# Solving RWKV's two right-hand sides in one run of products, loading two small weights a step ahead, and moving one merge behind the transitions

## The chip, the cores and the metric

One core of one Trainium2 chip runs the whole kernel. The metric is the device time of an execution in microseconds (us); lower is better. TensorE multiplies, DVE (VectorE) and ACT (ScalarE) read its results out of PSUM, POOL (GpSimd) does a little, SP (SyncE) issues most transfers.

## What is computed

A decoder block in float32 on 16 meta tokens and 1024 tokens of width 1024: a SwiGLU FFN at half step, a mixing stage, an output projection, a second FFN. The mixing stage adds two branches, A (gated DeltaNet, 8 heads of 128) and B (RWKV-7, 16 heads of 64). Cut to those:

```python
u = _rmsnorm(h, mix_norm[l])
aq, ak, av, az, abeta, aalpha, bcols, ga, gb = jnp.split(u @ w_in[l], ...)
# A, by chunks of 64 tokens:
tinv = lax.linalg.triangular_solve(m + eye, eye, left_side=True, lower=True, unit_diagonal=True)
# B, token by token (here also done by chunks of 64):
sa = jnp.einsum('bhvk,bhk->bhv', state, a_t)
state = state * w_t[:, :, None, :] + sa[..., None] * b_t[:, :, None, :] \
    + v_t[..., None] * k_t[:, :, None, :]
y_t = jnp.einsum('bhvk,bhk->bhv', state, r_t)
merged = jax.nn.sigmoid(ga) * o_a + jax.nn.sigmoid(gb) * o_b
h = h + merged @ w_out[l]
```

## The kernel before

The first FFN, the mixing stage, the output projection and the second FFN run one behind another. The mixing stage is done in two segments of the sequence (528 and 512 tokens) and in each of them in 8 steps; a step is one group of heads, one of A and two of B. 16 steps in all, numbered 0 to 15. Each step projects its inputs (the long products `pp`, 128x512, and `pw`, `pa` out of the small up-projection weights), then builds chunk operands, inverts small triangular matrices, and walks the chunks.

What is traced in which order stands in `schedule()`: a step's `merge_blocks`, `transitions`, `chains`, `gates` and `finish` are mixed with the next step's `operands` and `inverses` and with `new_b` and `new_a` of a later step. A list scheduler then sets each engine's order, so that work of several steps stands mixed in each queue, and each engine runs its queue strictly in that order.

Names that the text uses:

- `new_b`, `new_a` project; `gates` projects the output gates (`zg`). `new_b` loads `upr` (the up-projection weights of B) and `gates` loads `ugr` by SP and splits them on ACT and DVE into `upz` and `ug`. Any 128x1024 weight block is split in the same way into `w` (L159 on ACT, then L160 on DVE) once the block that was in the buffer has been read by its last `pp`.
- `operands`: `grb` are the score products of 64x128, which DVE masks into `LT`; `gra` those of A, which DVE makes into `UA` and `attn`; `bkt` transposes give `BKt`; the run `vp` gives `at` (a transposed AR) and `yb`; `ktp`, `btp` transpose for A and the meta tokens.
- `inverses` and `merge_blocks` invert by blocks into `Y`: the products `iv1` to `iv4`; iv3 gives `T64` through ACT, iv4 completes the inverse of A (the order prints all of them as iv with a number).
- `transitions` solves with B's part of `Y`: `xp` from `at` gives `xa`, `xp` from `LT`, `Vs` and then from that result gives `xv`, `vp` gives `vbk`. Then `mp` (matrices `mt` and `AR`, added up by DVE) and `np` (added to `vbk` and `yb` by DVE).
- `chains` walks the chunks (`b`, `p`, `pq`, `bm`, `am`).

Products with 64 rows and 64 columns use one quadrant of the array; where two quadrants on the diagonal are used, two run at a time. In the trace each float32 product of this kind has two records.

PSUM pools: `ch` has two banks, used in turn by xp, mp, np, iv and the transitions' vp; `mx` has two banks in the first segment and three in the second, used by `operands`. A tile there waits until the one before it in its bank has been read.

Of the kernel before, what the change touches and what calls it, by code (L numbers as in the profile page):

```python
# [185 lines left out]
BEFORE_SWITCH = "merge_blocks transitions operands+ inverses+ chains gates finish gates+ segment new_b++ new_a++"
SWITCH = "merge_blocks transitions operands+ inverses+ chains finish new_b++ new_a++"
LAST_BUT_ONE = "merge_blocks transitions operands+ inverses+ chains gates finish"
FINAL = "gates merge_blocks transitions chains fill finish"
# [1216 lines left out]
def transitions(g, q):  # L1406
# [3 lines left out]
    AR, LT, BKt, Vs, yb = q.AR, q.LT, q.BKt, q.Vs, ch3(q.yb, CB)  # L1410
    vbk = q.vbk = st.tile([P, NCB, CB], F32, name="vbk", tag="vbk")
    xa, xv = (st.tile([P, NCB, CB], F32, name=x, tag=x) for x in ("xa", "xv"))

    vka = q.at

    def solved(r):
        def f(i, h):
            t = tok(i, h)
            return Y[HS[t], i, HS[t]], r[HS[t], i], t, t
        return f  # L1420
# [7 lines left out]
    def va(i, h):  # L1428
        k = key(i, h)
        return LT[HS[k], i, 1 - (i & 1), :CB], Vs[HS[k], i], k, 1 - k  # L1430

    def vb(i, h):
        k = key(i, h)
        return BKt[HS[k], i, 1 - (i & 1)], Vs[HS[k], i], k, h
# [241 lines left out]
```

## Time and profile before

| | us |
|---|---|
| median of 3 runs | 3091.28 (3090.76 to 3095.39) |
| profiled execution | 3088.92 |
| its span, first to last instruction | 3087.2 |
| TensorE busy in the span | 2976.7 |

The profiled execution is the one that every row below comes from. A row of the timeline gives the start, the duration (of several alike: from the first's start to the last's end), the engine, the line, and what is written out of what; brackets give the engine's idle time just before it and what ended that. Busy times of TensorE rest on modelled ends of its instructions.

### The profile page before, as it was taken

How to read it: one execution, taken by the hardware profiler on the slowest of the kernel's cores; microseconds unless marked ns; L12 is line 12 of the kernel's file. 1: busy time of each engine (PE TensorE's matmuls, PEld its weight loads, DVE VectorE, ACT ScalarE, POOL GpSimd, SP SyncE). 2: the span in 40 equal slices, each digit the busy share in tenths (PEclk: the TensorE clock that was granted, in tenths of full speed). 3: DMA queues.
4: the chain of work that ended last, by engine and by line, in shares of the span. 5: the costliest groups of instructions: out<-in, count | busy, mean ns of one | idle time of the engine just before them, and what ended most of it. 6: DMA issues, size and time to landing. Idle time of an engine off the chain costs nothing.

```text
span 3087.2 us, 61391 instructions
## 1 busy us (share of the span) xinstructions
PE 2976.7 (96%) x25498; PEld 2538.9 (82%) x25498; DVE 1923.9 (62%) x3742; ACT 1326.2 (43%) x2308; POOL 330.3 (11%) x519
## 2 busy tenths in 40 slices
PE   8999999999899999999999999999999999999998
PEld 8999998998778888888777777777777888887886
DVE  6455453346667777677767777777766755555335
ACT  5322222126555645556565554555544432222114
POOL 0222220000000000000000000000000022332000
PEclk9999999999999999999999999999999999999999
DMA  3232224234223322233322232223345132224223
GB/s 126 80 97 83 83 86 157 79 100 140 62 74 77 81 71 70 73 79 88 93 78 73 78 87 82 73 71 85 101 134 190 64 102 89 82 82 170 86 77 114
DMA packets 257591, 287.17 MB, mean 93 GB/s; under 512 B 169296, under 2 KB 175440, under 8 KB 257312
## 3 DMA queue, kind: packets, MB, share of 16 engines
q1 hardware_dynamic: 253072, 271.43, 29.3%
q0 software_dynamic: 2512, 8.65, 0.7%
q8 instruction: 201, 3.29, 0.4%
q10 hardware_dynamic: 1728, 3.16, 0.3%
q14 instruction: 78, 0.64, 0.1%
HBM read 232.70 MB, written 50.47 MB: 92 GB/s over the span
## 4 chain that ended last, share of the span: by engine, by line
PE 58%; DVE 7%; ACT 5%; DMA 2%; issue 2%; SPq 1%; DVEq 0%; POOL 0%; ACTq 0%
PE pp L262 20%; PE pg L450 12%; PE pd L262 7%; PE pwo L262 2%; PE cs L1000 2%; PE pg L474 1%; PE b L1520 1%; PE vp L1035 1%; DVE w L160 1%; PE mp L1035 1%; PE gra L1230 1%; PE np L1035 1%; DVE acc L1151 1%; ACT w L159 1%; PE xp L1035 1%
## 5 line engine op out<-in xcount | busy, mean ns | idle before, releaser
L262 PE MATMUL pp<-uk,w 128*128 128x512 f32 (+2 forms) x4824 | 979.8, 351 | 5.4 <-DVE w L160 3.6
L262 PEld LDWEIGHTS pp<-uk,w 128*128 128x128 f32 x4824 | 742.0, 190 | 121.6 <-issue 32.2
L159 ACT ACTIVATE w<-wraw 128x1024 fp32r<-128x1024 f32 (+2 forms) x330 | 326.1, 989 | 723.5 <-PE pd L262 293.0
L262 PE MATMUL pd<-hd,w 128*128 128x512 f32 (+2 forms) x2640 | 498.5, 351 | 13.8 <-DVE w L160 9.8
L262 PEld LDWEIGHTS pd<-hd,w 128*128 128x128 f32 x2640 | 430.2, 190 | 81.0 <-DVE w L160 11.8
L160 DVE TENSOR_TENSOR w<-wraw,w 128x1024 fp32r<-128x1024 f32 (+2 forms) x330 | 376.1, 1140 | 88.4 <-ACT w L159 84.3
L450 PE MATMUL pg<-bt,w 128*128 128x256 f32 (+2 forms) x2520 | 404.0, 318 | 0.1
L456 DVE TENSOR_TENSOR c<-c,pg 128x520 f32<-128x520 f32 (+1 forms) x280 | 189.4, 690 | 336.2 <-PE pg L450 277.4
L450 PEld LDWEIGHTS pg<-bt,w 128*128 128x128 f32 x2520 | 361.1, 188 | 32.9 <-DVE w L160 0.3
L450 PE MATMUL pg<-b,w 128*128 128x256 f32 (+2 forms) x2160 | 348.1, 318 | 0.2 <-DVE c L456 0.2
L450 PEld LDWEIGHTS pg<-b,w 128*128 128x128 f32 x2160 | 309.9, 188 | 28.3 <-PE pg L450 0.4
L419 POOL TENSOR_TENSOR wrx<-wrx 128x512 f32<-128x512 f32 x38 | 57.2, 1504 | 759.0 <-DVE w22b L160 340.6
L1342 DVE TENSOR_TENSOR tb<-Ub,Xb 115x126 f32<-115x126 f32 (+22 forms) x496 | 124.9, 252 | 14.9 <-DMA Ub<-scr 6.4
L1344 DVE TENSOR_TENSOR Xb<-Xb,tb 115x126 f32<-115x126 f32 (+22 forms) x496 | 125.6, 253 | 9.3
L1151 DVE SCALAR_TENSOR_TENSOR acc<-xr,pk,acc 128x528 f32<-128x528 f32 (+1 forms) x144 | 109.2, 759 | 26.6 <-ACT acc L1147 24.9
L159 ACT ACTIVATE w<-wrx 128x1024 fp32r<-128x1024 f32 (+1 forms) x64 | 58.2, 909 | 157.0 <-PE pg L450 152.0
L609 DVE SCALAR_TENSOR_TENSOR h<-pd,h 128x528 f32<-128x528 f32 (+1 forms) x64 | 44.6, 699 | 118.8 <-PE pd L262 118.8
L609 DVE SCALAR_TENSOR_TENSOR hh<-pd,hh 128x512 f32<-128x512 f32 x64 | 44.2, 690 | 112.6 <-PE pd L262 108.7
L262 PE MATMUL pwo<-uk,w 128*128 128x512 f32 x384 | 98.2, 405 | 5.5 <-ACT uk L159 2.0
L918 ACT ACTIVATE sh<-pp,pk 128x528 f32<-128x528 f32 (+1 forms) x54 | 37.5, 694 | 126.1 <-PE pp L262 118.7
L262 PEld LDWEIGHTS pwo<-uk,w 128*128 128x128 f32 x384 | 71.6, 191 | 23.4 <-ACT uk L159 2.4
L159 ACT ACTIVATE hd<-hr 128x1040 fp32r<-128x1040 f32 (+1 forms) x44 | 45.3, 1060 | 67.4 <-DMA hr<-hid 42.5
(389 smaller groups left out, 3999.8 us busy)
## 6 DMA issues: line engine op xcount, KB each, us to landing
wraw<-in_win SPq DMA_DIRECT2D x150, 512.0 KB
wraw<-in_wgu SPq DMA_DIRECT2D x44, 512.0 KB
wrx<-in_wgu SPq DMA_DIRECT2D x44, 512.0 KB
wraw<-in_wdn SPq DMA_DIRECT2D x48, 320.0 KB
wraw<-in_wdn SPq DMA_DIRECT2D x32, 384.0 KB
hid<-c SPq DMA_DIRECT2D x44, 260.0 KB
hr<-hid SPq DMA_DIRECT2D x22, 520.0 KB
hid<-c SPq DMA_DIRECT2D x44, 256.0 KB
```

What stands on the lines that cost most here:

```text
L159: g.nc.scalar.activation(hi, src, AF.Copy)
L160: (eng or g.nc.vector).tensor_tensor(lo, src, hi.bitcast(F32), op=ALU.subtract)
L262: g.nc.tensor.matmul(ps, lhsT=l, rhs=r, start=i == 0, stop=i == n - 1)
L419: sums.tensor_tensor(a22, a21, a22, op=ALU.add)
L450: nc.tensor.matmul(ps[:, c0 : c0 + cn], lhsT=l[:, x, k, :], rhs=r[:, k, y, c0 : c0 + cn], start=i == 0, stop=i == 3 * HK - 1)
L456: nc.vector.tensor_tensor(o, x, y, op=ALU.add)
L609: nc.vector.scalar_tensor_tensor(hv, pd, 0.5, hv, op0=ALU.mult, op1=ALU.add)
L1000: nc.tensor.matmul(ps[:, :cn], lhsT=lhsT, rhs=sq[:, c0 : c0 + cn], start=True, stop=True)
L1035: g.nc.tensor.matmul(ps[e][HS[dst], c0 : c0 + CB], lhsT=l, rhs=r, start=True, stop=True)
L1151: nc.vector.scalar_tensor_tensor(acc[:, :n], xr[:, tap : tap + n], V("convw", ct * 4 + tap), acc[:, :n], op0=ALU.mult, op1=ALU.add)
L1342: nc.vector.tensor_tensor(tv, U[:, i, i + 1 :].unsqueeze(2).to_broadcast([npt, nt, ncc]), X[:, i, 0:ncc].unsqueeze(1).to_broadcast([npt, n ...
L1344: nc.vector.tensor_tensor(X[:, i + 1 :, 0:ncc], X[:, i + 1 :, 0:ncc], tv, op=ALU.add)
```

## The change

Four edits:

- `operands` now makes both right-hand sides of B's solve, side by side in one tile `rh`: the old `at` and the product of LT and Vs. It also makes the product of BKt and Vs into `vbk`. Both runs of products moved there from `transitions`, out of pool `ch` into `mx`.
- `transitions` solves both in one run `xp` of 16 products of 64x128 (before: 32 of 64x64 in two runs, one right-hand side behind the other) and two evictions of 128x512 into `xav` in place of four of 128x256.
- The up-projection weights of step n+1 are loaded when those of step n have been split, into tiles of their own (`upw_load`, `upw_next`).
- iv3, T64 and iv4 leave `merge_blocks` for `merge_a`, which is traced behind `transitions`.

`vbk` gets two buffers and `BKt` one, and a scratch of `finish` lies in AR in place of BKt.

```diff
-REGULAR = "merge_blocks transitions operands+ inverses+ chains gates finish new_b++ new_a++"
+REGULAR = "merge_blocks transitions merge_a operands+ inverses+ chains gates finish new_b++ new_a++"
...
+def upw_load(g, name, it):
+
+    if it < 2 * NJ:
+        raw = g.st.tile([P, 2, P], F32, name=name, tag=name)
+        g.nc.sync.dma_start(raw, g.a[name][it % NJ])
+        g.upw[name, it] = raw
...
-    raw = tmp("upr", 512).rearrange("p (a m) -> p a m", m=P)
-    nc.sync.dma_start(raw[:, 0:2, :], g.a["upwa"][j])
+    raw = upw_next(g, "upwa", it)
...
+    upw_load(g, "upwa", it + 1)
...
+    rh = q.rh = st.tile([P, NCB, 2, CB], F32, name="rh", tag="rh")
...
     for ps, cs in pa:
-        nc.scalar.activation(at[:, cs], ps, AF.Copy)
+        nc.scalar.activation(rh[:, cs, 0], ps, AF.Copy)
     for ps, cs in pr:
         nc.scalar.activation(ch3(yb, CB)[:, cs], ps, AF.Copy)
+    for ps, cs in run(g, g.mx, "vp", va)[0]:
+        nc.scalar.activation(rh[:, cs, 1], ps, AF.Copy)
+    for ps, cs in run(g, g.mx, "vp", vb)[0]:
+        nc.scalar.activation(vbk[:, cs], ps, AF.Copy)
...
+def merge_a(g, q):
...
     ps3 = g.ch.tile([P, 512], F32, name="iv3", tag="ch")
...
+    x = st.tile([P, NCB, 2, CB], F32, name="xav", tag="xav")
+    for cs in EO:
+        ps = g.ch.tile([P, 512], F32, name="xp", tag="ch")
+        for n, i in enumerate(range(cs.start, NCB, 2)):
+            for hp in HS:
+                nc.tensor.matmul(ps[hp, n * P : n * P + P], lhsT=Y[hp, i, hp],
+                                 rhs=q.rh[hp, i].rearrange("p a b -> p (a b)"), start=True, stop=True)
+        nc.scalar.activation(x[:, cs], ps.rearrange("p (c x b) -> p c x b", x=2, b=CB), AF.Copy)
...
-    px, pv = run(g, g.ch, "xp", solved(q.at), va)
-    for ps, cs in pv:
-        nc.scalar.activation(vka[:, cs], ps, AF.Copy)
-    for ps, cs in px:
-        nc.scalar.activation(xa[:, cs], ps, AF.Copy)
-    for ps, cs in run(g, g.ch, "xp", solved(vka))[0]:
-        nc.scalar.activation(xv[:, cs], ps, AF.Copy)
-    for ps, cs in run(g, g.ch, "vp", vb)[0]:
-        nc.scalar.activation(vbk[:, cs], ps, AF.Copy)
```

TensorE's queue around a step's transitions in the first segment, steps 1 to 5 alike (line numbers of the one kernel and of the other differ). Before:

```order
L1035 MATMUL xp<-at,Y_7139 64x64 x14
L1035 MATMUL vp<-Vs,BKt 64x64 x8
L1189 MATMUL grb<-AR,BK 64x128
L1035 MATMUL vp<-Vs,BKt 64x64 x8
L1035 MATMUL mp<-BKt,xa 64x64 x16
L1035 MATMUL mp<-LT,xa 64x64 x16
L1189 MATMUL grb<-AR,BK 64x128 x4
L262 MATMUL pp<-uk,w 128x512 x7
L1035 MATMUL np<-xv,BKt 64x64 x16
L1035 MATMUL np<-LT,xv 64x64 x16
L1189 MATMUL grb<-AR,BK 64x128 x16
L1476 MATMUL bm_13083<-uvm_7155,ltm 16x64 x2
```

and after:

```order
L1451 MATMUL xp<-rh,Y_7139 64x128 x7
L1038 MATMUL mp<-BKt,xav 64x64 x8
L1038 MATMUL mp<-LT,xav 64x64 x7
L1038 MATMUL mp<-BKt,xav 64x64 x8
L1038 MATMUL mp<-LT,xav 64x64 x9
L1204 MATMUL grb<-AR,BK 64x128 x16
L262 MATMUL pp<-uk,w 128x512
L1038 MATMUL np<-xav,BKt 64x64 x16
L1038 MATMUL np<-LT,xav 64x64 x16
L1204 MATMUL grb<-AR,BK 64x128 x16
L1430 MATMUL iv_12709<-XA,UA 64x64 x4
L262 MATMUL pp<-uk,w 128x512 x3
```

Seven pp and four grb stood between mp and np, now one pp and sixteen grb; the two merge products, which stood ahead of xp in before, now stand behind np where bm was.

DVE's queue in the same step. Before:

```order
L160 TENSOR_TENSOR w<-wraw,w 128x1024
L160 TENSOR_TENSOR ug<-ugr,ug 128x128
L1544 TENSOR_TENSOR ug<-ugr,ug 32x128
L1057 TENSOR_TENSOR upz<-upr,upz 64x128 x2
L1450 TENSOR_TENSOR mt<-mp,ck 64x4x64 x4
L1453 TENSOR_TENSOR AR<-mp,AR 128x4x64 x2
L1192 TENSOR_TENSOR LT<-grb,ck 128x4x128 x2
L1456 TENSOR_TENSOR vbk<-np,vbk 128x4x64 x2
L1459 TENSOR_TENSOR yb<-np,yb 128x4x64
L1457 TENSOR_TENSOR vbk<-vbk,gam 128x512
```

and after:

```order
L1233 TENSOR_TENSOR kts<-gp,tk 128x4
L1466 TENSOR_TENSOR mt<-mp,ck 64x4x64 x4
L1469 TENSOR_TENSOR AR<-mp,AR 128x4x64 x2
L1207 TENSOR_TENSOR LT<-grb,ck 128x4x128 x2
L160 TENSOR_TENSOR w<-wraw,w 128x1024
L1472 TENSOR_TENSOR vbk<-np,vbk 128x4x64 x2
L1475 TENSOR_TENSOR yb<-np,yb 128x4x64
L1473 TENSOR_TENSOR vbk<-vbk,gam 128x512
L1475 TENSOR_TENSOR yb<-np,yb 128x4x64
```

The split of a weight block into w, which DVE did ahead of mt, now stands between LT and the sum into vbk.

TensorE's queue in the second segment, steps 9 to 14 alike but for a few products. Before, from mp on:

```order
L1035 MATMUL mp<-LT,xa 64x64 x16
L1189 MATMUL grb<-AR,BK 64x128 x11
L1230 MATMUL gra<-kq 128x256 x2
L1035 MATMUL np<-xv,BKt 64x64 x16
L1035 MATMUL np<-LT,xv 64x64 x16
L1230 MATMUL gra<-kq 128x256 x2
L1259 MATMUL bkt<-ck,BK 64x64 x32
L1520 MATMUL b_22471<-SBs,mt 128x64
L1035 MATMUL vp<-ck,AR 64x64 x16
L1035 MATMUL vp<-LT,Vs 64x64 x16
L1285 MATMUL ktp<-ck,kq 128x128 x4
```

and after:

```order
L1038 MATMUL mp<-LT,xav 64x64 x9
L1204 MATMUL grb<-AR,BK 64x128 x17
L1038 MATMUL np<-xav,BKt 64x64 x16
L1038 MATMUL np<-LT,xav 64x64 x16
L1204 MATMUL grb<-AR,BK 64x128 x11
L1430 MATMUL iv_21975<-XA,UA 64x64 x4
L1204 MATMUL grb<-AR,BK 64x128 x4
L1435 MATMUL iv_21982<-Y_7139,T_21976 64x64 x4
L1245 MATMUL gra<-kq 128x256 x4
L1274 MATMUL bkt<-ck,BK 64x64 x32
L1038 MATMUL vp<-ck,AR 64x64 x16
```

Two gra left the gap between mp and np and grb came in; the merge products follow np, and two more runs of vp precede ktp.

ACT's queue at the transitions in the second segment. Before:

```order
L1440 ACTIVATE xa<-xp 128x4x64 x2
L1438 ACTIVATE at<-xp 128x4x64 x2
L159 ACTIVATE ug<-ugr 128x128
L1542 ACTIVATE ug<-ugr 128x128
L1055 ACTIVATE upz<-upr 128x256
L1442 ACTIVATE xv<-xp 128x4x64 x2
L1444 ACTIVATE vbk<-vp 128x4x64 x2
```

and after:

```order
L930 ACTIVATE zg<-pp 128x512
L159 ACTIVATE w<-wraw 128x1024
L1179 ACTIVATE Va<-vap 128x512
L1453 ACTIVATE xav<-xp 128x4x128
L1231 ACTIVATE E<-E 128x512
L1453 ACTIVATE xav<-xp 128x4x128
L1232 ACTIVATE eg<-gp 128x512
L1234 ACTIVATE kts<-kts 128x4
```

The splits of ug and upz no longer stand ahead of the eviction that the next products need; they now stand further down, in the chains.

TensorE's queue at `operands` in the first segment, from the end of the vp run on. Before:

```order
L1035 MATMUL vp<-LT,Vs 64x64 x16
L1500 MATMUL p_13109<-SA,kq 128x128
L262 MATMUL pp<-uk,w 128x512 x3
L1280 MATMUL btp<-ck,bkm 64x128
L1285 MATMUL ktp<-ck,kq 128x128 x4
```

and after:

```order
L1038 MATMUL vp<-LT,Vs 64x64 x16
L1516 MATMUL p_13077<-SA,kq 128x128
L262 MATMUL pp<-uk,w 128x512 x3
L1038 MATMUL vp<-Vs,LT 64x64 x16
L1038 MATMUL vp<-Vs,BKt 64x64 x8
L1520 MATMUL p_13081<-rhA,Y_7139 128x128
L1038 MATMUL vp<-Vs,BKt 64x64 x8
L1309 MATMUL btp<-ck,bkm 64x128
L1524 MATMUL pq<-kq,SA 128x128
L1525 MATMUL pq<-attn,vn 128x128
L1314 MATMUL ktp<-ck,kq 128x128 x4
```

LT times Vs and BKt times Vs stand between vp and btp, with p of the chains in between.

## Rows read from the trace of the kernel before

**Rows 1.** Page, part 1: busy time, share of the span, instructions

```profile
PE 2976.7 (96%) x25498; PEld 2538.9 (82%) x25498; DVE 1923.9 (62%) x3742; ACT 1326.2 (43%) x2308; POOL 330.3 (11%) x519
```

**Rows 2.** Stretches: us, each engine's busy time (instructions), PEclk, DMA share, GB/s

```profile
978.30:1460.90 482.60, 470.45 (x5637) 400.04 (x5636) 352.19 (x865) 265.54 (x546) 30.10 (x115) 1.00 0.28 75
...
1677.10:2289.40 612.30, 584.55 (x6436) 460.12 (x6435) 452.90 (x1081) 331.02 (x635) 39.19 (x99) 0.99 0.31 85
```

**Rows 3.** Waits of PE: line waited for, total us, times, longest

```profile
PE vp L1035 <- ACT xv L1442: 12.1, 14, 2.4
...
PE xp L1035 <- ACT at L1438: 7.7, 14, 0.9
...
PE np L1035 <- DVE AR L1453: 6.1, 13, 1.5
...
PE vp L1035 <- DVE attn L1234: 3.7, 5, 1.1
```

**Rows 4.** Groups by form, PE: records | busy us, mean ns | idle before

```profile
L1189 PE MATMUL grb<-AR,BK 64*64 64x128 f32 x1024 | 59.5, 282 | 0.0
...
L1035 PE MATMUL xp<-at,Y 64*64 64x64 f32 x1024 | 39.7, 222 | 7.8 <-ACT at L1438 7.7
```

**Rows 5.** Timeline of PE, transitions of a step in the first segment

```profile
1271.33 0.27 PE L1035 MATMUL xp<-at,Y 64*64 64x64 f32 x2 [0.89 <-ACT at L1438]
...
1273.46 0.68 PE L1035 MATMUL vp<-Vs,BKt 64*64 64x64 f32 x16 [0.25 <-ACT xv L1442]
...
1275.92 1.88 PE L262 MATMUL pp<-uk,w 128*128 128x512 f32 x7
1278.06 0.86 PE L1035 MATMUL np<-xv,BKt 64*64 64x64 f32 x27 [0.25 <-DVE AR L1453]
...
1279.49 1.09 PE L1189 MATMUL grb<-AR,BK 64*64 64x128 f32 x28
1280.79 0.38 PE L1476 MATMUL bm<-uvm,ltm 16*16 16x64 f32 x4 [0.21 <-DVE yb L1459]
```

**Rows 6.** Timeline of DVE, the same step

```profile
1271.05 1.23 DVE L160 TENSOR_TENSOR w<-wraw,w 128x1024 fp32r<-128x1024 f32 x1 [0.78 <-ACT w L159]
...
1275.74 1.73 DVE L1450 TENSOR_TENSOR mt<-mp,ck 64x256 f32<-64x256 f32 x4 [2.37 <-PE mp L1035]
1277.48 0.76 DVE L1453 TENSOR_TENSOR AR<-mp,AR 128x256 f32<-128x256 f32 x2
1278.16 1.28 DVE L1192 TENSOR_TENSOR LT<-grb,ck 128x512 f32<-128x512 f32 x2
1279.56 0.76 DVE L1456 TENSOR_TENSOR vbk<-np,vbk 128x256 f32<-128x256 f32 x2
1280.23 0.42 DVE L1459 TENSOR_TENSOR yb<-np,yb 128x256 f32<-128x256 f32 x1
1280.56 0.68 DVE L1457 TENSOR_TENSOR vbk<-vbk,gam 128x512 f32<-128x512 f32 x1
```

**Rows 7.** Timeline of ACT, that step's operands: evictions behind the vp run

```profile
1292.20 0.66 ACT L1274 ACTIVATE at<-vp 128x256 f32<-128x256 f32 x2 [1.50 <-PE vp L1035]
1292.74 0.67 ACT L1276 ACTIVATE yb<-vp 128x256 f32<-128x256 f32 x2
```

**Rows 8.** Timeline of ACT, transitions of a step in the second segment

```profile
1948.83 0.31 ACT L159 ACTIVATE ug<-ugr 128x128 fp32r<-128x128 f32 x1 [1.83 <-DMA ugr<-in_upg]
...
1949.55 0.64 ACT L1442 ACTIVATE xv<-xp 128x256 f32<-128x256 f32 x2
```

**Rows 9.** Timeline of PE, the same step

```profile
1950.24 0.68 PE L1035 MATMUL vp<-Vs,BKt 64*64 64x64 f32 x16 [1.59 <-ACT xv L1442]
...
1953.14 1.13 PE L1230 MATMUL gra<-kq 128*128 128x256 f32 x4
1954.83 0.86 PE L1035 MATMUL np<-xv,BKt 64*64 64x64 f32 x27 [0.56 <-DVE AR L1453]
...
1959.61 0.88 PE L1035 MATMUL vp<-ck,AR 64*64 64x64 f32 x30 [0.78 <-DVE attn L1234]
```

**Rows 10.** Timeline of PE, the step behind the switch of segments

```profile
1687.50 0.97 PE L1035 MATMUL np<-xv,BKt 64*64 64x64 f32 x27 [1.46 <-DVE AR L1453]
```

More of the change, by code (lines that the diff above doesn't have):

```diff
@@ L184 @@
 FIRST = "new_b new_a operands inverses", "new_b new_a"
-REGULAR = "merge_blocks transitions operands+ inverses+ chains gates finish new_b++ new_a++"
[L186 to L189, printed above, removed]
+REGULAR = "merge_blocks transitions merge_a operands+ inverses+ chains gates finish new_b++ new_a++"
+BEFORE_SWITCH = "merge_blocks transitions merge_a operands+ inverses+ chains gates finish gates+ segment new_b++ new_a++"
+SWITCH = "merge_blocks transitions merge_a operands+ inverses+ chains finish new_b++ new_a++"
+LAST_BUT_ONE = "merge_blocks transitions merge_a operands+ inverses+ chains gates finish"
+FINAL = "gates merge_blocks transitions merge_a chains fill finish"
 def weight_order():
@@ L816, in middle @@
             nc.gpsimd.memset(t, 0.0)
+        g.upw = {}
+        for name in ("upwa", "upg"):
+            upw_load(g, name, 0)
         steps = {}
@@ L1037, in run, with upw_next @@
     return out
+def upw_load(g, name, it):
[3 more added lines that the diff above has]
+        g.upw[name, it] = raw
+def upw_next(g, name, it):
+    return g.upw.pop((name, it))
 def new_b(g, it):
@@ L1251, in operands @@
     inverse_inputs(g, q)
-    BKt = q.BKt = st.tile([P, NCB, 2, CB], F32, name="BKt", tag="BKt", bufs=2)
+    BKt = q.BKt = st.tile([P, NCB, 2, CB], F32, name="BKt", tag="BKt")
     ident = g.C("ident")
@@ L1270, in vr, with vb @@
         return Vs[HS[k], i], LT[HS[k], i, 1 - (i & 1), CB:], k, h
+    def vb(i, h):
+        k = key(i, h)
+        return BKt[HS[k], i, 1 - (i & 1)], Vs[HS[k], i], k, h
+    yb = q.yb = st.tile([P, FULL], F32, name="yb", tag="yb", bufs=2)
+    vbk = q.vbk = st.tile([P, NCB, CB], F32, name="vbk", tag="vbk", bufs=2)
     pa, pr = run(g, g.mx, "vp", lambda i, h: (AR[HS[h], i, 0, :], ident[HS[h], HS[h]], h, tok(i, h)), vr)
     for ps, cs in pa:
-        nc.scalar.activation(at[:, cs], ps, AF.Copy)
+        nc.scalar.activation(rh[:, cs, 0], ps, AF.Copy)
     for ps, cs in pr:
         nc.scalar.activation(ch3(yb, CB)[:, cs], ps, AF.Copy)
+    for ps, cs in run(g, g.mx, "vp", va)[0]:
+        nc.scalar.activation(rh[:, cs, 1], ps, AF.Copy)
+    for ps, cs in run(g, g.mx, "vp", vb)[0]:
+        nc.scalar.activation(vbk[:, cs], ps, AF.Copy)
     if meta:
@@ L1409, in transitions @@
     Y = g.Y[q.it % 2]
[L1410 to L1420, printed above, removed]
+    AR, LT, BKt = q.AR, q.LT, q.BKt
+    vbk, yb = q.vbk, ch3(q.yb, CB)
+    x = st.tile([P, NCB, 2, CB], F32, name="xav", tag="xav")
[6 more added lines that the diff above has]
+        nc.scalar.activation(x[:, cs], ps.rearrange("p (c x b) -> p c x b", x=2, b=CB), AF.Copy)
     def by_tok(l, r):
@@ L1426, in by_tok @@
         return f
[L1428 to L1434, printed above, removed]
-    px, pv = run(g, g.ch, "xp", solved(q.at), va)
-    for ps, cs in pv:
-        nc.scalar.activation(vka[:, cs], ps, AF.Copy)
-    for ps, cs in px:
-        nc.scalar.activation(xa[:, cs], ps, AF.Copy)
-    for ps, cs in run(g, g.ch, "xp", solved(vka))[0]:
-        nc.scalar.activation(xv[:, cs], ps, AF.Copy)
-    for ps, cs in run(g, g.ch, "vp", vb)[0]:
-        nc.scalar.activation(vbk[:, cs], ps, AF.Copy)
     bt = lambda r, i: BKt[r, i, i & 1]
     br = lambda r, i: LT[r, i, i & 1, CB:]
-    pm, pr = run(g, g.ch, "mp", by_tok(lambda r, i: xa[r, i], bt), by_tok(lambda r, i: xa[r, i], br))
+    pm, pr = run(g, g.ch, "mp", by_tok(lambda r, i: x[r, i, 0], bt), by_tok(lambda r, i: x[r, i, 0], br))
     for ps, cs in pm:
@@ L1453, in transitions @@
         nc.vector.tensor_tensor(AR[:, cs, 1, :], ps, AR[:, cs, 1, :], op=ALU.add)
-    pn, py = run(g, g.ch, "np", by_tok(bt, lambda r, i: xv[r, i]), by_tok(lambda r, i: xv[r, i], br))
+    pn, py = run(g, g.ch, "np", by_tok(bt, lambda r, i: x[r, i, 1]), by_tok(lambda r, i: x[r, i, 1], br))
     for ps, cs in pn:
@@ L1572, in finish @@
     nc.vector.scalar_tensor_tensor(oa, oa, V("aog"), zg, op0=ALU.mult, op1=ALU.mult)
-    sq = q.BKt[:, 0:4].rearrange("p c y m -> p (c y m)")
+    sq = q.AR[:, 0:4].rearrange("p c y m -> p (c y m)")
     rg = st.tile([P, FULL], F32, name="rg", tag="ro")
```

12 lines of the change are left out of this document (8 added, 4 removed).

## The prediction

> **What bounds the kernel now.** First the busy times [rows 1]: TensorE works in 2976.7 of 3087.2 us, 96%. Then the stretches [rows 2]: from 978 to 1461 us (five steps of the first segment, about 96.5 us each) it is busy 470.45 of 482.60, from 1677 to 2289 us (seven steps of the second, 87.5 us each) 584.55 of 612.30, at a granted clock of 1.00 and 0.99 (the 2.4 GHz level). So the time is TensorE's instruction stream plus the moments in which its queue stands, 2.4 us a step in the first segment (12.15 / 5) and 4.0 in the second (27.75 / 7). DVE and ACT matter only where they release it. Then the waits of PE by what ended them [rows 3]: vp behind the eviction of xv 12.1 us, xp behind the eviction of `at` 7.7, np behind AR 6.1, vp behind attn 3.7. The change aims at the first two. Last the timeline of one step of each segment [rows 5 to 9], since every edit reorders the queue there.
>
> **The product itself.** 32 products of 64x64 become 16 of 64x128: the same columns. The two operand quadrants that xp uses are the diagonal ones, in before and after. Over the run 512 products xp<-at (two records each) show 39.7 us of busy time and 512 of 64x128 (grb) 59.5 [rows 4], 78 and 116 ns each: by these 32 x 78 = 2.5 us become 16 x 116 = 1.9, 0.6 a step. But grb has all four quadrants to run in and overlaps other work less or more, and the xp rows hold the stretches where grb is mixed in. I take 0.1 a step saved, and 0.6 as the low end. mp now runs bank by bank, which on the diagonal quadrants costs a little; I put the PE work of a step at +0.1 (-0.5 to +0.2).
> By the Trainium skill, page "TensorEngine Tiling (Array Packing)", section "Instruction Overhead", a matmul costs as much as some 60 columns whatever is below that. By it 64 columns stand just above the floor and halving the count saves nothing; the 0.6 of the busy rows would need a floor well above 64. The trace does not decide it, and my sum takes 0.1.
>
> **First segment, a step (1 to 5 alike).** Removed: the second xp run's wait for `at`, 0.89, and the second vp's wait for xv, 0.25 [rows 5].
> Between mp and np: np may start only when DVE has added mt and AR out of mp's banks, since the pool has two. mt starts at 1275.74, np at 1278.06 [rows 5, 6]: 2.32 us, and in the one step where only fifteen small products stand between, np waits 1.46 [rows 10]. That gap is fixed by DVE, so what counts is how much work stands in it. Before, 4 grb and 7 pp, and 0.25 is left over; after, 16 grb and 1 pp. Six pp go out (7 took 1.88 with the last one's 0.5, so 0.23 each, 1.38), twelve grb come in (28 records in 1.09, so 0.06 a product, 0.72) [rows 5]. The pp are done elsewhere, so TensorE loses 1.38 - 0.72 = **+0.66**.
> Behind np: where bm stood after 16 grb, waiting 0.21 for the first yb [rows 5], now stands the third merge product (iv3), which needs the same yb because that frees its bank. But DVE now has the split of a weight block between LT and vbk; before, it had been done at 1271.05, ahead of mt, in 1.23 us [rows 6]. LT ends at 1279.44, the split would end at 1280.65, and vbk, which started at 1279.56, starts there: **+1.1**. Everything behind iv3 on PE (pp, iv4, bm) waits with it. Then iv4 waits for ACT's T64: 0.3 to start, 0.33 for the eviction (as one of the pair of 128x256 evictions, 0.66 [rows 7]) and 0.15 back, against three pp (0.69): **+0.15** (0 to 0.35).
> Second bank of mp behind ACT's second xav, with Va and E queued between the two evictions: a first eviction is covered by vap and 7 xp, the second by 15 mp only. **+0.2** (0 to 0.5), no row of before shows it.
> In `operands`, LT Vs and BKt Vs now run out of the pool that holds two banks. The first follows p1 and three pp, where btp stood without a wait, by which time three of the four evictions of 1292.20 to 1293.41 are done [rows 7]: no wait. The second half of BKt Vs needs both evictions behind LT Vs (0.25 + 0.66 + 0.15 = 1.06) with 8 products and p2 to cover it (0.6): 0.4; ktp needs that half's own eviction (0.25 + 0.38 + 0.15 = 0.78, covered by btp and pq, 0.25): 0.5. Together **+0.8** (0.3 to 1.1; the nearest rows are those evictions). Their products and evictions themselves only move from the transitions.
> By the same page's section "PSUM Bottleneck", packed products speed up TensorE but not the evacuation, which may become the bottleneck. By it the four runs would follow their evictions one by one, with 1.06 for each run of two, 0.3 a step more than I take and about 4 us in all. The trace leans the other way, as four evictions fit behind two runs [rows 7], and I keep 0.8.
> Sum: 0.1 + 0.66 + 1.1 + 0.15 + 0.2 + 0.8 - 0.89 - 0.25 = **+1.9 a step**, +0.3 to +3. Five such steps 9.4; step 6 has two more pp ahead of iv3, +1.4; step 0 has no split there and five pp left before np, -0.3. **First segment +10.5.**
>
> **Second segment, a step.** The xv wait is here: ACT holds the splits of ug and upz, which wait for a load (1.83 us at 1948.83), ahead of xv at 1949.55 [rows 8], and vp waits 1.59 [rows 9]. The prefetch ends that whole kind: 12.1 less 6 x 0.25 of the first segment leaves 10.6 over eight transitions, about 1.7 a step over the six regular ones. Also gone: xp behind `at`, 0.34 a step by the rest of 7.7, and vp behind attn, 0.78 at 1959.61 [rows 9], 0.6 on average of 3.7, because gra moves ahead of bkt.
> New: between mp and np stood 11 grb and 2 gra (1.13 for four records [rows 9], about 0.47 a product) with 0.56 of wait [rows 9]; now 17 grb alone: 0.94 out, 0.36 in, **+0.6**. iv3 waits for yb: from np's start 1954.83 DVE has LT 1.28, zg (nearest row the 128x512 sum, 0.68 [rows 6]), two vbk 0.67 and yb 0.33, so iv3 at 1958.0, against np 1.1 and 11 grb 0.66 (1956.6): **+1.3**. iv4 behind T64 with 4 grb to cover it: **+0.5**. The operands' evictions with three banks: **+0.5** (0.1 to 0.8), vp behind BKt +0.2, mp's second bank +0.1.
> Sum: 3.2 - 0.34 - 1.7 - 0.6 = **+0.55 a step** (-0.5 to +1.2), six steps **+3.3**. The step at the switch, the one behind it and the last I leave at zero (each loses and gains such waits; plus or minus 3).
>
> **Loads.** Loading ahead puts on SP's queue a transfer that waits for the splits of the current weights; the weight blocks behind it wait too. Its cover is that weight blocks are loaded ahead and DMA is idle over two thirds (share 0.28 and 0.31 [rows 2]). I cost it at nothing; if a block comes late it is a few us in all, in the range's upper part. Ahead of the middle stage and behind it nothing moves.
>
> **Sum.** 10.5 + 3.3 = about +14 us on the profiled execution's 3088.92 (span 3087.2 and 1.7 around it), 3103. That execution is 2.4 us under the median 3091.28, so the median goes to **3105 us**, +0.45%. A difference under 0.2% (6.2 us) can't be told from none.
>
> **Rivals.**
> *Faster, about 3072.* The removed waits are worth 7.7 + 12.1 = 19.8 us; if the new ones don't appear, 3091.3 - 19.8 = 3072. That needs DVE to be earlier: mt's adds starting on mp's first bank, of which after has 15 of the 16 products done before the second bank's begin, and the weight split not standing there when yb is due. For it: DVE is idle between its bursts. Against: mt's first add comes behind all of mp in before too, and 1.46 us of wait with little filler [rows 10] is the price of that very situation. 0.15.
> *No change, about 3092.* The low ends hold: product 0.5 shorter, evictions covered, so +0.3 a step in the first segment (2 us) and -0.2 in the second (-1). 0.22.
> *Slower still, about 3115.* Upper ends, +2.7 a step in the first and +1.2 in the second segment: 16 + 7. 0.13, on the same side as my forecast.
> *The forecast*, 3098 to 3111: 0.50. It is decided by the two waits at np and iv3 alone: 3 us of new idle a step in the first segment against 1.14 removed.
>
> **How the numbers follow.** Slower by over 0.2%: 0.50 + 0.13, less a little for a forecast's lower edge: 0.62. Within: 0.21. Faster: 0.17, the rival and the lower tail of no change. The range leaves out most of the faster case and a little on top: 3078 to 3116.
>
> **What would show it.** PE's waits of after: none of vp or ug behind a load; a wait of np behind AR of about 0.9 a step in the first segment and 1.2 in the second; a wait of iv3 behind yb near 1.3 in both, with the weight split on DVE directly ahead of vbk in the first; small ones of vp and ktp behind ACT. I am wrong if iv3 finds yb done, if mt starts before mp's last products, or if the xp run takes over half a microsecond less than before. If the first segment's step stays at 96.5 us, its part of the sum is wrong; if the second's falls under 87, the prefetch was worth more than I took.

## The result and the profile after

| | before | after |
|---|---|---|
| median, us | 3091.28 (3085.38 to 3096.28, 9 runs) | 3103.28 (3097.63 to 3108.27, 9 runs) |
| ratio | | 1.0041, 95% interval 1.0031 to 1.0051 |
| profiled execution, its span, us | 3088.92, 3087.2 | 3107.74, 3106.0 |

The changed kernel is slower by 0.41%, where +0.45% was forecast. Its profiled execution lies 4.5 us above its median and that of before 2.4 below, so of the 18.8 us between the two spans 12 stand for the medians.

Page of after, part 1 (busy time, share of the span, instructions), which answers [rows 1]:

```profile
PE 3001.4 (97%) x24986; PEld 2554.1 (82%) x24986; DVE 1918.4 (62%) x3742; ACT 1321.8 (43%) x2276; POOL 338.4 (11%) x519
```

TensorE's idle time is 3106.0 - 3001.4 = 104.6 us, before 3087.2 - 2976.7 = 110.5. So in total it does not wait more; it is busy 24.7 us longer, with 512 records fewer, at a granted clock of 0.989 where before had 0.992. Waits of PE of after by the line waited for (total us, times, longest), against [rows 3]:

```profile
PE np L1038 <- DVE AR L1469: 16.4, 14, 1.4
PE iv L1430 <- DVE yb L1475: 13.5, 14, 1.1
...
PE vp L1038 <- ACT BKt L1277: 2.7, 9, 0.3
...
PE iv L1435 <- ACT T L1432: 2.0, 7, 0.5
...
PE vp L1038 <- ACT yb L1301: 1.0, 1, 1.0
```

The rows of xv, `at` and attn (23.5 us in before) are gone. np behind AR rose from 6.1 to 16.4, and iv3 behind yb is new. A step of the first segment, timeline of PE of after (against [rows 5]):

```profile
1077.49 0.43 PE L1451 MATMUL xp<-rh,Y 64*64 64x128 f32 x2
1077.85 0.73 PE L262 MATMUL pp<-uk,w 128*128 128x512 f32 x2
1078.51 1.09 PE L1451 MATMUL xp<-rh,Y 64*64 64x128 f32 x16
1079.53 0.66 PE L1178 MATMUL vap<-ck,acc 128*128 128x128 f32 x4
1080.12 0.39 PE L1183 MATMUL vmp<-ck,acc 128*16 128x128 f32 x2
1080.44 0.97 PE L1451 MATMUL xp<-rh,Y 64*64 64x128 f32 x13
...
1084.17 0.50 PE L262 MATMUL pp<-uk,w 128*128 128x512 f32 x1
1085.62 0.86 PE L1038 MATMUL np<-xav,BKt 64*64 64x64 f32 x26 [0.95 <-DVE AR L1469]
...
1089.28 0.73 PE L1430 MATMUL iv<-XA,UA 64*64 64x64 f32 x8 [1.13 <-DVE yb L1475]
```

and DVE's in the same step (against [rows 6]):

```profile
1083.31 1.73 DVE L1466 TENSOR_TENSOR mt<-mp,ck 64x256 f32<-64x256 f32 x4 [3.54 <-PE mp L1038]
1085.05 0.76 DVE L1469 TENSOR_TENSOR AR<-mp,AR 128x256 f32<-128x256 f32 x2
1085.72 1.28 DVE L1207 TENSOR_TENSOR LT<-grb,ck 128x512 f32<-128x512 f32 x2
1086.92 1.22 DVE L160 TENSOR_TENSOR w<-wraw,w 128x1024 fp32r<-128x1024 f32 x1
1088.05 0.75 DVE L1472 TENSOR_TENSOR vbk<-np,vbk 128x256 f32<-128x256 f32 x2
1088.71 0.41 DVE L1475 TENSOR_TENSOR yb<-np,yb 128x256 f32<-128x256 f32 x1
```

From mt's start to np's it is again 2.31 us (2.32 before). np waits 0.95 with sixteen grb and one pp as filler. The split of w stands ahead of vbk, and iv3 waits 1.13 for the yb behind it. In the second segment the same two waits, PE:

```profile
1969.72 0.86 PE L1038 MATMUL np<-xav,BKt 64*64 64x64 f32 x26 [1.35 <-DVE AR L1469]
...
1972.84 0.52 PE L1430 MATMUL iv<-XA,UA 64*64 64x64 f32 x5 [0.98 <-DVE yb L1475]
```

The five regular steps of the first segment as one stretch (us, then each engine's busy time and instructions, granted clock, DMA share, GB/s), before and then after:

```profile
988.50:1471.00 482.50, 470.39 (x5630) 399.95 (x5631) 353.01 (x866) 265.15 (x544) 30.10 (x115) 1.00 0.29 77
```

```profile
987.90:1481.80 493.90, 479.48 (x5472) 406.21 (x5472) 349.10 (x866) 266.57 (x536) 34.72 (x115) 0.99 0.29 75
...
1077.50:1175.40 97.90, 94.96 (x1095) 80.59 (x1094) 69.88 (x174) 53.30 (x109) 6.91 (x23) 1.00 0.28 73
1175.40:1274.80 99.40, 96.47 (x1095) 81.75 (x1094) 69.86 (x174) 53.32 (x109) 6.93 (x23) 0.98 0.27 72
1274.80:1375.70 100.90, 98.10 (x1095) 82.71 (x1094) 69.71 (x174) 53.28 (x109) 7.08 (x23) 0.97 0.27 71
```

+11.4 us over five steps. Two of them, with the same instructions as their neighbours, lost 1.5 and 3.0 us at a granted clock of 0.98 and 0.97. At a clock of 1.00 a step takes 97.8 to 97.9 instead of 96.5: +1.35, of which +0.9 is busy time (94.96, before 470.39 / 5 = 94.08) and under 0.5 idle.

### The profile page after: what moved, and what is told of

It reads as the page before. It is cut to its first block, busy times and chain, and to the rows that moved or that the text cites. A ratio compares the mean times of both kernels' runs of the same rounds, so it can differ in the third digit from the quotient of the medians.

```text
span 3106.0 us, 60313 instructions
## 1 busy us (share of the span) xinstructions
PE 3001.4 (97%) x24986; PEld 2554.1 (82%) x24986; DVE 1918.4 (62%) x3742; ACT 1321.8 (43%) x2276; POOL 338.4 (11%) x519
## 4 chain that ended last, share of the span: by engine, by line
PE 61%; DVE 8%; ACT 4%; issue 2%; DMA 1%; SPq 0%; DVEq 0%; ACTq 0%; POOL 0%
PE pp L262 21%; PE pg L450 12%; PE pd L262 7%; PE pwo L262 2%; PE cs L1003 2%; PE pg L474 1%; PE vp L1038 1%; PE xp L1451 1%; PE gra L1245 1%; PE b L1536 1%; DVE w L160 1%; PE mp L1038 1%; PE bkt L1274 1%; DVE mt L1466 1%; ACT w L159 1%
```

## The experiments

My theory: the loss is made by the two new waits at np and iv3, both on banks that DVE frees late. Rivals: another edit of the bundle makes it; or the total is no sum of waits at all. In the kernels built from before I write p, s, m for the three edits: prefetch, solve in one run, merge moved behind the transitions.

| edits | run | median, us | ratio to before (95%) |
|---|---|---|---|
| p | e1_prefetch | 3085.49 | 0.9974 (0.9961 to 0.9987) |
| s | e2_solve | 3084.35 | 0.9972 (0.9962 to 0.9983) |
| m | e3_merge | 3101.00 | 1.0017 (1.0006 to 1.0029) |
| p, s | e4_no_merge | 3074.75 | 0.9939 (0.9926 to 0.9952) |
| s, m | e9_solve_and_merge | 3126.38 | 1.0106 (1.0089 to 1.0122) |
| p, m | e10_prefetch_and_merge | 3102.94 | 1.0036 (1.0023 to 1.0050) |
| p, s, m | the changed kernel | 3103.28 | 1.0041 (1.0031 to 1.0051) |

### One edit alone

**The loads a step ahead**, in the kernel before:

```diff
-    raw = tmp("upr", 512).rearrange("p (a m) -> p a m", m=P)
-    nc.sync.dma_start(raw[:, 0:2, :], g.a["upwa"][j])
+    raw = upw_next(g, "upwa", it)
...
+    upw_load(g, "upwa", it + 1)
```

> The kernel before with one edit: the up-projection weights are loaded a step ahead. Theory: the eviction of xv no longer stands behind a load on ACT, so PE's wait of vp behind xv falls from 12.1 us to some 1.5 to 3 (the first segment's share stays), and the time falls by 8 to 10 us, to about 3082. Rival: the wait is only a cover for another one that ends a moment later (xp's own evictions or the second products), so vp's wait falls but others rise by as much, and the time stays within 3 us of 3091.

Ratio 0.9974, about -8 us. Its wait of vp behind xv, against 12.1 in [rows 3]:

```profile
PE vp L1038 <- ACT xv L1457: 3.5, 14, 0.4
```

The waits of 1.6 us behind a load are gone; behind rhA, p now waits 5.9 us (1.0 before). The term of 1.7 a step in the forecast, for the prefetch, was of this size.

**The solve in one run**, with the products that it needs in `operands`, in the kernel before (lines as in the change's diff):

```diff
+    for ps, cs in run(g, g.mx, "vp", va)[0]:
+        nc.scalar.activation(rh[:, cs, 1], ps, AF.Copy)
...
+    for cs in EO:
+        ps = g.ch.tile([P, 512], F32, name="xp", tag="ch")
...
-    px, pv = run(g, g.ch, "xp", solved(q.at), va)
```

> The kernel before with the batched solve alone (both right-hand sides in one run of 64x128 products, LT Vs and BKt Vs made in operands; merge and loads as before). Theory: xp's wait behind at and vp's behind xv go (19.8 us in all), but most of the filler leaves the gap between mp and np in the first segment (11 grb and 1 pp in place of 4 grb and 7 pp), so np's wait rises from 6.1 to about 16 us, and operands get waits of a few us; with the xv wait gone here too the time lies within 5 us of 3091. Rival (the batching is the gain of this change): 3076 to 3083, with np's wait not above 8 us.

3084.35 us, ratio 0.9972: between my two cases. Its two largest waits inside the steps:

```profile
PE np L1035 <- DVE AR L1449: 17.4, 15, 2.8
PE bm L1472 <- DVE yb L1455: 8.6, 7, 1.3
```

np's wait rises as the theory says, and bm takes the wait for yb, since the splits of ug and upz stand between LT and vbk on DVE here. Yet the kernel is faster: the waits for `at` and xv are gone. The gain lies in the second segment, where the five steps from the np of step 9 to that of step 14 take 446.2 us in place of 453.3; those of the first take 486.2 in place of 482.5. The group of xp by form in this kernel, against [rows 4]:

```profile
L1431 PE MATMUL xp<-rh,Y 64*64 64x128 f32 x512 | 32.0, 274 | 0.0
```

39.7 to 32.0 us of busy time for the same columns, but TensorE hardly gains by it. The busy time of a group runs to the modelled end of the last record of each run, and other products have started by then. What counts is the time from start to start, in before and then here:

```profile
1268.09 0.92 PE L1035 MATMUL xp<-at,Y 64*64 64x64 f32 x25
1268.81 0.27 PE L1035 MATMUL xp<-Vs,LT 64*64 64x64 f32 x2
```

```profile
1076.43 1.72 PE L1431 MATMUL xp<-rh,Y 64*64 64x128 f32 x28
1077.98 0.38 PE L1189 MATMUL grb<-AR,BK 64*64 64x128 f32 x2
```

Before, 25 records take 1268.81 - 1268.09 = 0.72 us, 0.029 each; here 28 take 1077.98 - 1076.43 = 1.55, 0.055 each. At these rates the 64 old records of a step come to 1.84 us and the 32 new ones to 1.77 (estimates): the run saves less than 0.1 us a step.

**The merge's move**, in the kernel before:

```diff
-REGULAR = "merge_blocks transitions operands+ inverses+ chains gates finish new_b++ new_a++"
+REGULAR = "merge_blocks transitions merge_a operands+ inverses+ chains gates finish new_b++ new_a++"
...
+def merge_a(g, q):
```

> The kernel before with one edit: iv3, T64 and iv4 traced behind the transitions. Theory: the gap between mp and np keeps 3 grb and 8 pp in the first segment, so np's wait stays near 6 us; iv3 takes bm's place behind np and waits for yb, but the weight block's split is not ahead of it on DVE here, so that wait is 0.2 to 0.5 us a step, 5 us in all; the time is 3091 to 3098. Rival (the move of the merge alone costs what the whole change lost): 3101 to 3106, with iv3's wait behind yb at 12 us or more.

3101.00 us, ratio 1.0017. The time is that of the rival, but without its condition: iv3 waits only 3.1 us behind yb. The profiled execution is the fastest of its twelve, 12 us under their median, so its rows show the least of it. Its five steps of the first segment:

```profile
985.40:1475.50 490.10, 474.35 (x5636) 398.86 (x5635) 354.89 (x865) 265.51 (x544) 36.63 (x115) 1.00 0.29 75
```

TensorE is busy 4.0 us longer than before at a clock of 1.00, and the stretch 7.6 longer. The move costs something by itself.

### Two edits

**Without the merge's move**: the changed kernel with iv3, T64 and iv4 back in `merge_blocks`.

```diff
-REGULAR = "merge_blocks transitions merge_a operands+ inverses+ chains gates finish new_b++ new_a++"
+REGULAR = "merge_blocks transitions operands+ inverses+ chains gates finish new_b++ new_a++"
...
-def merge_a(g, q):
-    nc, st, UA, XA = g.nc, g.st, q.UA, g.XA
-    Y = g.Y[q.it % 2]
     ps3 = g.ch.tile([P, 512], F32, name="iv3", tag="ch")
```

> The changed kernel with the merge back ahead of the transitions, so batched solve and prefetch alone. Theory: the wait of iv3 behind yb (13.5 us) goes, np's wait stays at 14 to 17 us, xp waits for nothing; 3103 less about 11 gives 3089 to 3095. Rival (the solve is at fault, by slower products and operands' waits): 3100 or more.

3074.75 us, 0.9939: far below what I had expected, and 28.5 us under the changed kernel. Its waits, and its five steps:

```profile
PE np L1038 <- DVE AR L1464: 9.0, 15, 1.0
...
PE bm L1487 <- DVE yb L1470: 1.5, 2, 1.3
```

```profile
987.90:1466.80 478.90, 470.43 (x5471) 401.51 (x5472) 347.46 (x866) 267.00 (x535) 30.15 (x115) 1.00 0.29 78
```

A step takes 95.8 us, under before's 96.5, with before's busy time. DVE in a step of it:

```profile
1080.08 1.22 DVE L160 TENSOR_TENSOR w<-wraw,w 128x1024 fp32r<-128x1024 f32 x1 [0.73 <-ACT w L159]
1081.22 1.72 DVE L1461 TENSOR_TENSOR mt<-mp,ck 64x256 f32<-64x256 f32 x4
```

The split of w is ahead of mt again, as in [rows 6]. So with the solve in, it was the merge's move that brought it behind LT; without the solve (e3_merge, e10_prefetch_and_merge) nothing stands there between LT and vbk in the first segment. Prefetch and solve together are a gain, and the loss of the whole change comes with the merge's move.

**The prefetch and the merge's move**, without the solve (the diffs of e1_prefetch and e3_merge together).

> The kernel before with the loads a step ahead and the moved merge, the solve as before. Theory: additive, -8 and +5: 3086 to 3092, iv3's wait behind yb below 5 us, since mp and np keep their filler of pp. Rival (the merge behind the transitions costs 20 us wherever ACT is rid of the loads): 3100 or more.

1.0036, so the prefetch gains nothing once the merge is moved. Adding up the effects of single edits (0.9974 and 1.0017) fails. iv3 waits for yb only 2.2 us in the whole run here, so that wait is not needed for a loss. What is longer than in e1_prefetch is TensorE's busy time, 2998.5 us against 2981.8; its idle time is 100.3 against 104.2. The five steps:

```profile
991.90:1480.30 488.40, 472.55 (x5632) 397.41 (x5633) 353.81 (x868) 265.98 (x545) 34.60 (x115) 1.00 0.29 76
```

**The solve and the merge's move**, without the prefetch:

```diff
-    raw = upw_next(g, "upwa", it)
+    raw = tmp("upr", 512).rearrange("p (a m) -> p a m", m=P)
+    nc.sync.dma_start(raw[:, 0:2, :], g.a["upwa"][j])
...
```

> The changed kernel without the loads a step ahead: batched solve and moved merge. Theory: the loss comes from these two together (with the solve batched, np follows mp with hardly any filler and the merge products then wait behind np), so the time is far above the sum of the two alone (solve -8, merge +5): 3100 to 3112, with iv3's wait behind yb at 10 us or more. Rival (the two are additive and the prefetch is what disturbs the order): 3086 to 3093.

1.0106, 3126.38 us, slower than I expected. In both segments the splits of ug stand between LT and vbk on DVE, in front of the yb that iv3 needs. Its two largest waits inside the steps:

```profile
PE iv L1415 <- DVE yb L1460: 19.3, 15, 1.4
PE np L1035 <- DVE AR L1454: 16.7, 15, 1.4
```

That is 5.8 us more at iv3 than in the changed kernel; the 23 us between the two medians are more than the listed waits hold. Part goes with the clock: its five steps of the first segment were granted 0.97 and took 506.3 us, and over all its executions the granted clock is 0.986 on average, 0.990 in the changed kernel.

### The mechanism

**The merge products in other banks**: the changed kernel with iv3 and iv4 out of pool `mx`.

```diff
-    ps3 = g.ch.tile([P, 512], F32, name="iv3", tag="ch")
+    ps3 = g.mx.tile([P, 512], F32, name="iv3", tag="mx")
...
-    ps4 = g.ch.tile([P, 512], F32, name="iv4", tag="ch")
+    ps4 = g.mx.tile([P, 512], F32, name="iv4", tag="mx")
```

> The changed kernel with iv3's and iv4's results in the operands' PSUM banks in place of the transitions'. They need no yb then and are scheduled between mp and np. Theory: iv3's wait behind yb (13.5 us) goes and the gap before np gets filler, so np's wait of 16.4 falls by a third or more; 3080 to 3090. Rival (the place of the merge behind xp costs by itself, by what it does to xp and the projections): 3097 or more.

3082.48 us, 0.9965. The scheduler now puts them between mp and np, where filler was short. PE in a step of the first segment:

```profile
1078.87 0.71 PE L1430 MATMUL iv<-XA,UA 64*64 64x64 f32 x8
1079.51 0.96 PE L262 MATMUL pp<-uk,w 128*128 128x512 f32 x3
1080.40 0.50 PE L1435 MATMUL iv<-Y,T 64*64 64x64 f32 x5
...
1081.51 0.73 PE L1038 MATMUL np<-xav,BKt 64*64 64x64 f32 x29
```

Neither iv3 nor np waits here. iv3 no longer needs a bank that yb frees, and iv3 and iv4 are now filler ahead of np; bm and p wait 4.3 us behind yb in their place. Some 24 us (0.0076 of the ratio) are back. The run changes the bank and with it the order, and does not part the two.

Over the whole span TensorE is idle 81.7 us here, 104.6 in the changed kernel and 89.2 in e4_no_merge; it is busy 2999.2, 3001.4 and 2983.3. So the other banks give back the idle time that the merge's move brought, and hardly anything of the busy time. The rest against e4_no_merge, 0.0026 or 8 us, is in that busy time, and I read part of it from xp. Groups of xp by form, first e4_no_merge, then this kernel; the changed kernel's row is the same as the second:

```profile
L1446 PE MATMUL xp<-rh,Y 64*64 64x128 f32 x512 | 32.2, 274 | 0.0
```

```profile
L1451 PE MATMUL xp<-rh,Y 64*64 64x128 f32 x512 | 41.2, 277 | 0.0
```

In every kernel with the solve, these 512 records are busy 9 us longer where the merge has been moved. In e4_no_merge they run nearly unbroken:

```profile
1077.26 1.72 PE L1446 MATMUL xp<-rh,Y 64*64 64x128 f32 x28
1078.81 0.38 PE L1204 MATMUL grb<-AR,BK 64*64 64x128 f32 x2
```

28 records in 1078.81 - 1077.26 = 1.55 us, 0.055 each. In after (timeline above) xp is cut by pp and by vap, products of the full array: the first two records take 1077.85 - 1077.49 = 0.36 until pp starts, 0.25 more than two such; the next sixteen 1.02 until vap, 0.14 more; and the two pp between take 0.66 until the next xp starts, against 0.23 each in [rows 5], 0.20 more. So each of these three changes between quadrant products and full-array ones cost 0.14 to 0.25 us, 0.59 in this step, and over sixteen steps like it that would be 9 us (an estimate). That this makes the remaining 8 us is read from rows; no run isolated it.

**The last gate block's split on POOL** in place of DVE:

```diff
-    split(g, raw[:, :kk, :], w[:, 0, :kk, :], w[:, 1, :kk, :])
+    pool = name == "win" and 67 <= idx[0] < 75
+    split(g, raw[:, :kk, :], w[:, 0, :kk, :], w[:, 1, :kk, :], eng=g.nc.gpsimd if pool else None)
```

> The changed kernel, but the second half of one weight block's split per step (that of the last gate projection, the one that DVE has between LT and vbk in the first segment) is done by POOL; PE's order stays nearly the same. Theory: iv3 waits for yb because this split of 1.2 us stands ahead of vbk, so in steps 1 to 5 iv3's wait falls from 1.13 to some 0.3 (it comes five grb earlier here), np's wait stays at 0.95; about 4 to 6 us in all: 3097 to 3100. Rival (iv3's wait comes from np itself, or POOL is too slow for the block): 3102 or more.

3117.75 us, 1.0082: slower, where I had expected a gain. The local part held. PE in a step of the first segment:

```profile
1088.18 0.52 PE L1431 MATMUL iv<-XA,UA 64*64 64x64 f32 x5 [0.37 <-DVE yb L1476]
...
1089.38 0.50 PE L1436 MATMUL iv<-Y,T 64*64 64x64 f32 x5 [0.46 <-ACT T L1433]
```

iv3 waits 0.37 in place of 1.13, so the split is what held yb up in this step; but iv4 behind T64 takes 0.46 of it back. In the whole run iv3's wait behind yb falls only from 13.5 to 11.5 us (one of them is 2.9, behind the np ahead of the switch of segments), mp behind xav waits 6.6, and the distance at the switch is 146.8 us from np to np, 139.9 in after. The split takes POOL 2.37 us where DVE took 1.22, and DVE's vbk of 128x512 beside it takes 1.19 in place of 0.68. Shortening one wait did not shorten the kernel.

**DVE's additions bank by bank**, so that the first bank comes free sooner:

```diff
...
-    for ps, cs in pn:
+    for (ps, cs), (pt, ct) in zip(pn, py):
         nc.vector.tensor_tensor(vbk[:, cs], ps, vbk[:, cs], op=ALU.add)
+        nc.vector.tensor_tensor(yb[:, ct], pt, yb[:, ct], op=ALU.add)
...
```

> The changed kernel with DVE's additions behind mp and np done bank by bank (mt and AR of the first bank, then of the second; vbk and yb likewise); the scheduler then runs np bank by bank and puts LT and the weight split behind yb. Theory: the first half of np is released 1.0 us earlier and yb comes right behind np, so iv3's wait falls below 0.3 a step and np's total stays or falls a little; 3086 to 3094. Rival (the waits come from somewhere else than DVE's chain): 3100 or more.

3096.09 us, 1.0010, a little above what I expected. The wait at iv3 ends, part of it reappears at iv4:

```profile
PE np L1038 <- DVE AR L1468: 11.0, 15, 1.2
...
PE iv L1435 <- ACT T L1432: 3.5, 14, 0.3
```

5.4 us less at np and 13.3 less at iv3, 1.5 more at iv4: 17 us of listed waits for a ratio 0.0031 (10 us) lower. Against that np itself, now run bank by bank, got longer: its two groups by form are busy 21.8 and 20.9 us, 16.2 and 12.8 in after.

**The merge traced behind `operands`** of the next step:

```diff
-REGULAR = "merge_blocks transitions merge_a operands+ inverses+ chains gates finish new_b++ new_a++"
+REGULAR = "merge_blocks transitions operands+ merge_a inverses+ chains gates finish new_b++ new_a++"
...
```

> The changed kernel with the merge traced one action later, behind operands. Theory: iv3 still stands behind np and takes a bank from it, and DVE's row in the first segment is unchanged, so the first segment's steps stay near 98 us; in the second, gra moves ahead of iv3, which covers some of its wait; 3095 to 3106. Rival (the position in the source decides): 3085 or less.

1.0032 (1.0020 to 1.0043), not to be told from the changed kernel. np waits the same 16.4 us; at iv3 6.8 are left, in six steps in place of fourteen. Halving that wait moved nothing that can be measured.

### Toward a better kernel

**Additions bank by bank without the merge's move**, the diff of e7_banks_in_turn on e4_no_merge:

> Batched solve and prefetch with the merge back in its old place (3075 by itself) and DVE's additions bank by bank. Theory: the remaining wait of np behind AR, 9.0 us, falls by half: 3067 to 3073. Rival: the halves of np wait one behind the other and lose what the first gains: 3074 to 3078.

3080.31 us, 0.9962 (0.9949 to 0.9974): above both of my cases and 0.0023 above e4_no_merge, the two intervals just overlapping. np waits 8.6 us in place of 9.0, so next to nothing was won. What got longer is again np run bank by bank, 21.8 and 20.3 us in its groups by form against 16.2 and 12.8; TensorE's busy time in the five steps is 474.90 in place of 470.43.

**Less DVE work ahead of np**, on e4_no_merge: half of mt's additions become ACT copies, and POOL adds the identity.

```diff
+    h0, h1 = HS
     for ps, cs in pm:
-        for hp in HS:
-            nc.vector.tensor_tensor(g.mt[hp, cs, hp], ps[hp], g.C("ident")[hp, hp].unsqueeze(1).to_broadcast([CB, NCB // 2, CB]),
-                                    op=ALU.add)
+        nc.vector.tensor_tensor(g.mt[h0, cs, h0], ps[h0], g.C("ident")[h0, h0].unsqueeze(1).to_broadcast([CB, NCB // 2, CB]),
+                                op=ALU.add)
+        nc.scalar.activation(g.mt[h1, cs, h1], ps[h1], AF.Copy)
+    nc.gpsimd.tensor_tensor(g.mt[h1, :, h1], g.mt[h1, :, h1], g.C("ident")[h1, h1].unsqueeze(1).to_broadcast([CB, NCB, CB]),
+                            op=ALU.add)
```

> Batched solve and prefetch with the merge in its old place (3075 by itself), and half of mt's additions taken off DVE: ACT copies that half out of PSUM and POOL adds the identity later. Theory: the banks of mp come free 0.9 us earlier, so np's wait behind AR, 9.0 us in all, falls below 3 us, for 6 to 9 us: 3066 to 3070. Rival (np then waits for ACT, or the time goes where the halves of np did in the run with the banks in turn): 3074 or more.

np's wait falls from 9.0 to 3.7 us, where I expected below 3, but the time only to 3072.18 (0.9936, 0.9922 to 0.9950), short of the 3066 to 3070 that I expected and not to be told from e4_no_merge:

```profile
PE np L1038 <- DVE AR L1467: 3.7, 8, 0.6
```

Both beat the kernel before by 0.6% and the changed one by a full per cent.

## Why the prediction was right, and where its steps were not

**Sign and the two waits: right.** np was forecast to wait about 0.9 a step in the first segment and 1.2 in the second: 0.95 and 1.35 in the timelines. iv3: 1.1 to 1.3, measured 1.13 and 0.98, with the w split ahead of vbk in the first segment and zg there in the second, as told. The removed waits went as told: 23.5 us.

**The size: in part luck.** The forecast's 14 us were nearly all idle time of TensorE. In the two profiled executions its idle time fell by 5.9 us and its busy time rose by 24.7, a part of that with the clock. Of the 18.8 us between the two spans, by the distances between successive np, the five steps of the first segment gave +11.4 (9.4 forecast), of which 4.5 came with the lower clock of two steps. The distance at the switch, from the np of step 6 to that of step 7, gave +5.3 (139.9 against 134.6 us), where I had 1.4 for step 6 and nothing for the switch. The granted clock of that stretch is 0.96, before 0.99, and pp waits 4.2 us there behind gg of DVE, a wait that e2_solve has too (3.4) and before has not. The two distances behind it gave +1.9, which I had left at zero, and the stretch from the np of step 14 to the end +3.3, where I had 0.55 for that step. The five regular distances of the second segment gave -2.6. So the total agrees better than its parts.

**First segment, +1.9 a step forecast, +1.35 measured at full clock, by other terms.** Of this forecast +1.8 was idle time. The listed waits give np 0.95 - 0.25, iv3 1.13, bm -0.21, xp -0.89, vp -0.25: +0.5, as do the windows. The **evictions** term (0.8) was over-sized: in these five steps the waits have no row of vp or ktp behind ACT, and in the whole run the two wait 4.3 us behind ACT, 0.9 before (xv apart). By the Trainium skill, page "TensorEngine Tiling (Array Packing)", section "PSUM Bottleneck", evacuation may become the bottleneck once packing has made TensorE four times as fast. The trace does not show it here. mp's second bank (0.2 in the whole run) and iv4 behind T64 (2.0) were over-sized too.

**The product's term, +0.1, was right for the product and left out something else.** From start to start the 64x128 products save less than 0.1 us a step (e2_solve), which is the 0.1 that I took and not the 0.6 of the busy rows. By the Trainium skill, page "TensorEngine Tiling (Array Packing)", section "Instruction Overhead", a product of one column takes as long as one of 60; by it 64 columns lie just above the floor, and halving the number of products saves nothing. The rows agree: 0.029 us for a record of 64x64, 0.055 for one of 64x128. But TensorE's busy time rose 0.9 a step, outside the -0.5 to +0.2 that I gave. It goes with the merge's move, which leaves xp to be cut by full-array products; e4_no_merge has the old busy time with the new products. That this is all of it is not shown: with the merge unmoved and xp uncut, the five steps are busy 474.90 us in e8_no_merge_banks and 475.19 in e12_less_dve_before_np, and with the merge moved 471.65 in e11_merge_later. I had no term for it: I counted what stands in a gap, not how often the kind of product changes.

**Second segment, +0.55 a step forecast, -0.5 measured.** The five steps from the np of step 9 to that of step 14 went from 453.3 to 450.7 us, just below the -0.5 to +1.2 a step that I gave. TensorE is as busy there as before (434.00 and 433.97), so it is the waits. By the rows of these stretches, a step gained np 0.9 (0.6 forecast), iv3 1.0 (1.3), iv4 0.3 (0.5) and vp and ktp behind ACT 0.3 (0.7). It lost xv 1.9 (1.7), `at` 0.3, attn 0.5 (0.6), and 0.5 of b behind SBs, for which I had no term. The terms that I gave for iv3 add up to 1957.8 and not to 1958.0, +1.2 in place of +1.3.

**Where my reading was wrong as a whole**: I priced the change as one reordering. The rival "faster, 3072" was thought to need an earlier DVE; two of the three edits without the third give just that time, 3074.75. Its second condition held there: no weight split in front of yb. Its first, mt ahead of mp's last products, held in the first segment too (mt at 1081.22, mp's last at 1081.51), but np came no sooner behind mt, 2.31 us as before, and still waits 9.0 us. One reading was off without effect: in the step of [rows 10], 57 records of bkt, about 28 products, stand between mp and np, not fifteen.

**What stays open**: why the merge's move costs 0.0134 with the solve alone, 0.0062 with the prefetch alone and 0.0102 with both, where the listed waits and busy rows of the profiles account only roughly. By one profile of each kernel, TensorE's busy time rises with the move in every pair, by 14.4 us alone, 16.7 with the prefetch, 18.1 with both and 32.8 with the solve, there at a granted clock of 0.985 against 0.991. Its idle time rises only with the solve in, by 9.5 and with the prefetch too by 15.4; without the solve it falls, by 14.4 and 3.9. Open is also what makes the granted clock fall to 0.97 in single steps.

## What to carry to other kernels

Price each edit of a bundle alone, and once more with each of the others: here two gains and a loss that grows with them made a small loss of the whole. A product that is moved takes a PSUM bank and a place: look up which run used the bank before, which engine frees it, and what stands ahead of that on the engine's queue, and try another pool. Time a run of products from start to start: the busy time of its group in the profile counts ends that other products overlap. A wait that is shortened is not time won until the next one is known: of the ways tried here to shorten one, only other banks paid nearly in full.
